# SyncE's transfers in the written order through the attention stage of a hybrid encoder block

## The chip, the cores and the metric

The kernel runs on one core of a Trainium2 chip. The metric is the device time of one execution in microseconds (us). A core has five engines with queues of their own: TensorE (PE; its weight loads are shown apart as PEld), VectorE (DVE), ScalarE (ACT), GpSimd (POOL) and SyncE (SP), which computes nothing and here issues nearly all DMA transfers. Each engine runs its instructions in the order of its queue: where one waits for a semaphore, what stands behind it waits too.

## What is computed

One layer on x of 2048 tokens by 1024, cut to its core:

```python
h = rmsnorm(x, norm_mix_g)
proj = h @ w_in                              # u_ssm 512 | q 512 | k 512 | v 512
y_ssm = s5_mixer(u_ssm, ...)                 # diagonal complex state space, GELU, GLU
y_att = chunked_attention(q, k, v, rel_bias) # 8 heads of 64; a chunk of 64 tokens sees
                                             # itself and the 8 chunks before it
x = x + concat(rmsnorm(y_ssm), rmsnorm(y_att)) @ w_out
x = x + (silu(h2 @ w_gate) * (h2 @ w_up)) @ w_down     # h2 = rmsnorm(x), 2816 wide
return rmsnorm(x, norm_final_g)
```

Products that need float32 accuracy are made of three: each operand is kept as a rounded part and a remainder (hi, lo), and hi*hi, hi*lo and lo*hi are added (`mm3`).

## The kernel before

The program is written for a framework that takes the instructions in the order in which Python emits them, and then schedules each engine's queue with a timing model: an instruction that is ready earlier by the model may be put ahead of its written place. Buffers are named pools with a number of slots; a tile that needs a slot waits for the last use of the tile that had it. `keep_in_program_order` pins an instruction behind the one that was emitted before it on its engine. `Ordered` (line 68) does so for all matmuls, so PE runs in written order. `Pinned` (81) wraps another engine in the same way: `k.V`, `k.A`, `k.Q` are the pinned DVE, ACT and SP; `nc.vector`, `nc.scalar`, `nc.sync` are the free ones.

The stages: projection of u (`u_phase`, with `ssm_prologue` beside it), attention with the state-space units beside it (`att_phase`, the one that changes), the mix and output projection (`mix_phase`), and the feed-forward part (`gate_up_phase`, `down_phase`).

`att_phase` works on 4 blocks of 512 tokens (sb 0 to 3). Its loop (line 956) runs 128 steps and a few more; step s = 32 sb + 8 pr + 4 hh + qp handles head 2 pr + hh and the tile qp of 128 queries. In a step are emitted, in this order: the scores of step s (two or four matmuls, tile `sc`), the transposes of step s-2, at the end of a head its product with v, and then the next pieces of the *units*, which prepare what later steps need. A unit is a Python generator, advanced so that its pieces spread evenly over a given range of steps; it is started two to four steps earlier, so that its first loads are asked for. For block sb, counted from step 32 sb:

- `hT_unit`: loads 8 input tiles (`xt`, 256 KB each, 2 buffers, line 722), normalises them on DVE (736), and makes hi on ACT (737) and lo on DVE (728). Tiles 0 to 2 start at -14, tiles 3 to 7 at -10, with their first two loads; from -8 on they take the buffers of the block before, which PE reads until about step -9.
- `qk_unit` (q and k of a pair of heads; from steps -8, 2, 7 and 19) and `v_unit` (v of four heads; from -2 and 13). Each uses two weights `w` of 1 MB, in 3 buffers. In block 0 they are loaded raw, split (ACT, DVE) and stored to `wss`; later blocks load them from there (705). They are asked for at -11, 32 sb + 0, 5 and 17 for `qk_unit` and at -4 and 11 for `v_unit`.
- q of a pair goes from PSUM to `q2h` and `q2l` (777, 778; 3 buffers, one for each head), and a copy by DMA fills their other half (779, 780). k goes to `k2`, is stored (`ks`, 785) for the next block, and the part of `k2` with the block before's keys, the *kept keys*, is loaded (755).
- A bias tile `nb` (320 KB) is loaded for the next head in each step with qp = 2 (825). The result of a pair of heads is stored as `ya_s` (907) at steps 3, 11, 19, 27.
- Eight `ssm_unit`s, every 14 steps, load `U`, `Bst`, `Tm`, `Vm` in many small transfers (568), scan on POOL, and store `y` (660).

At step 119 (`OPEN`, line 957) buffers are released and the first part of `mix_phase` joins as one more unit. In `weight_steps` (line 1277), far behind, four DRAM-to-DRAM copies of 512 KB of w_down into `wt` go through `k.Q`.

Of SP's instructions in `att_phase` before the change, those of state-space unit 0, of `hT_unit` for block 0 and of weights 0 and 4 are pinned; the rest are free.

Of the kernel before, what the change touches and what calls it, by code (L numbers as in the profile page):

```python
# [16 lines left out]
P = 128  # L17
# [3 lines left out]
NG, CH, NS = 32, 16, 64  # L21
# [58 lines left out]

class Pinned:


    def __init__(self, tc, eng):
        self.tc, self.eng = tc, eng

    def __getattr__(self, name):
        f = getattr(self.eng, name)
        return lambda *a, **b: self.tc.keep_in_program_order(f(*a, **b))  # L89


class K:
    def __init__(self, tc, io):
        self.tc, self.nc, self.io = tc, tc.nc, io
        self.n = 0
        self.te = Ordered(tc)
        self.ta = self.te if PINA else tc.nc.tensor
        self.V, self.A, self.Q = (Pinned(tc, e) for e in (tc.nc.vector, tc.nc.scalar, tc.nc.sync))
# [9 lines left out]
def f32(ap):  # L108
    return ap.bitcast(F32)
# [451 lines left out]
def ssm_unit(k, p, psum, S, b, eng):  # L561
# [3 lines left out]
    U = k.t(p, "U", [P, GB, NC], bufs=2)  # L565

    def load(out, in_):
        ins = nc.sync.dma_start(out, in_)
        if b == 0:
            k.tc.keep_in_program_order(ins)  # L570

    for j in range(L):
        load(U[j * CH : (j + 1) * CH], S["u"][b * F : (b + 1) * F, j, :].rearrange("(g c) t -> c g t", c=CH))
# [77 lines left out]
    for q in range(GP):  # L651
        ps = k.t(psum, "pj", [P, 2, NC], bufs=2)
        for g2 in range(2):
            g = 2 * q + g2
            k.ta.matmul(ps[:, g2, :], tm[:, g, :], U[:, g, :], start=True, stop=False)
            k.ta.matmul(ps[:, g2, :], vm[:, g, :], XG[:, g, :], start=False, stop=True)
        nc.scalar.copy(Y[:, 2 * q : 2 * q + 2, :], ps[:])
        if q == GP - 1:
            for j in range(L):
                nc.sync.dma_start(S["y"][b * F : (b + 1) * F, j, :].rearrange("(g c) t -> c g t", c=CH), Y[j * CH : (j + 1) * CH])  # L660
        yield


# [25 lines left out]
def att_phase(k, ident, S):  # L689
    tc, nc, io = k.tc, k.nc, k.io  # L690
    with ExitStack() as cx:
# [3 lines left out]
        def load_w(sb, n):  # L695

            w = k.t(aw, "w", [P, 2, 1024], F32R, bufs=WB)
            if sb == 0:
                raw = k.t(aw, "raw", [P, 1024], bufs=2)
                pin = n in (0, 4)  # L700
                (k.Q if pin else nc.sync).dma_start(raw[:], io["w_qk"][n] if n < 8 else io["w_v"][n - 8])
                split(k, w[:, 0], w[:, 1], raw[:], k.V if pin else k.wlo_eng, k.A if pin else None)
                keep[n] = w
            else:
                nc.sync.dma_start(f32(w[:]), S["ws"][n])
            return w[:, 0], w[:, 1]

        def keep_w(n):
            if n in keep:
                (k.Q if n in (0, 4) else nc.sync).dma_start(S["ws"][n], f32(keep.pop(n)[:]))  # L710

        def hT_unit(sb, q0=0, q1=KT):
            hi, lo = hT.setdefault(sb, ([], []))
            ts = slice(sb * SB, (sb + 1) * SB)
            xts = {}
            V, A, Q = (k.V, k.A, k.Q) if sb == 0 else (nc.vector, nc.scalar, nc.sync)

            def load(q):
                if q < q1:
                    x = RING[q] if sb == 0 and q < 2 * DB else None  # L720
                    xts[q] = k.t(aw, x, [P, SB]) if x else k.t(aw, "xt", [P, SB], bufs=XB)
                    Q.dma_start(xts[q][:], io["xt"][q * P : (q + 1) * P, ts])

            ahead = 2 if sb else KT
            for q in range(q0, q0 + ahead):
                load(q)
            def low(q):
                V.tensor_tensor(lo[q][:], xts[q][:], f32(hi[q][:]), op=ALU.subtract)

            for q in range(q0, q1):  # L730
                yield
                load(q + ahead)
                xt = xts[q]
                for v, n in zip(hT[sb], ("hi", "lo")):
                    v.append(k.t(aw, f"{n}{q}x" if q < DB and sb % 2 else f"{n}{q}", [P, SB], F32R))
                V.scalar_tensor_tensor(xt[:], xt[:], k.gm[:, q : q + 1], S["rsn"][:, ts], op0=ALU.mult, op1=ALU.mult)
                A.copy(hi[q][:], xt[:])  # L737
                if sb == 0 and q:
                    low(q - 1)
                if sb or q == KT - 1:  # L740
                    low(q)
            yield

        def qk_unit(sb, pr):
# [5 lines left out]
            else:  # L750
                ts = [(k.t(aa, "q2h", [P, SB], F32R, bufs=3), k.t(aa, "q2l", [P, SB], F32R, bufs=3), k.t(aa, "k2", [P, 2 * SB], F32R, bufs=3)) for _ in range(2)]
            qk[sb, pr] = ts
            if sb > 0:
                for hh in range(2):
                    nc.sync.dma_start(f32(ts[hh][2][:, :SB]), S["k"][(sb - 1) % 2, 2 * pr + hh])
            both = (sb, pr) == (0, 0)
            pss = []
            for c in range(2):
                if c == 0 or not both:
                    cc = range(2) if both else (c,)  # L760
                    pss += [k.t(pfs, "pf", [P, 512]) for _ in cc]
                    for q in range(KT):
                        cs = slice(q * P, (q + 1) * P)
                        for m in cc:
                            wh, wl = ws[m]
                            mm3(k.ta, pss[m][:], wh[:, cs], wl[:, cs], hi[q][:], lo[q][:], q == 0, q == KT - 1)
                            if q == 2:
                                keep_w(4 * m + pr)
                        if q < KT - 1:
                            yield  # L770
                ps = pss[c]
                for hh in range(2):
                    q2h, q2l, k2 = ts[hh]
                    a = slice(hh * 64, hh * 64 + 64)
                    o = slice(64 - hh * 64, 128 - hh * 64)
                    if c == 0:
                        nc.scalar.activation(q2h[a, :], ps[a, :], AF.Copy, scale=-0.125)
                        nc.vector.scalar_tensor_tensor(q2l[a, :], ps[a, :], -0.125, f32(q2h[a, :]), op0=ALU.mult, op1=ALU.subtract)
                        nc.sync.dma_start(f32(q2h[o, :]), f32(q2h[a, :]))
                        nc.sync.dma_start(f32(q2l[o, :]), f32(q2l[a, :]))  # L780
                    else:
                        nc.scalar.copy(k2[a, -SB:], ps[a, :])
                        nc.vector.tensor_tensor(k2[o, -SB:], ps[a, :], f32(k2[a, -SB:]), op=ALU.subtract)
                        if sb < NSB - 1:
                            nc.sync.dma_start(S["k"][sb % 2, 2 * pr + hh], f32(k2[:, -SB:]))
                yield

        QK_N = 1 + 2 * KT
# [110 lines left out]
        def pv_scale(st):  # L899
# [7 lines left out]
            nc.sync.dma_start(S["ya"][sb, pr * P : (pr + 1) * P, :], ya[:])  # L907
# [798 lines left out]
```

## Time and profile before

| | |
|---|---|
| median of the three runs shown | 2344.45 us |
| the three runs | 2341.79, 2353.02, 2344.45 us |
| the profiled execution, its own time | 2347.47 us |
| its span, first to last instruction | 2345.7 us |
| mean granted PE clock | 0.969 |
| attention steps 0 to 127, first score matmuls | 142.5 to 770.8 us |

The profile is of one execution. A row of the timeline reads: start in us from the span's start, length in us, engine (SPq is SP's queue), source line, operation, output tile <- input tiles, shape, count of merged instructions, and in brackets the idle time of the engine before it and what ended it. Line 75 is the helper `Ordered.matmul`, so all of PE's matmuls bear it, and line 89 that of `Pinned`. The chain of work that ended last is followed back from the end; its rows give start, length and what ran, a transfer from its issue to its landing. A row of the waits reads: who waited, for whom, us in total, number of times, longest. SP's own waits are counted from the end of its instruction before.

### The profile page before, as it was taken

Reading aid. Unit: us, or ns where it says so; the run is one execution under the profiler, and the core shown is the slowest. Engines: PE = TensorE matmul, PEld = TensorE weight load, DVE = VectorE, ACT = ScalarE, POOL = GpSimd, SP = SyncE. Lnnn points to the kernel's source line nnn. Section 1 sums busy time; section 2 is a strip of 40 time slices with the busy share of each in tenths; the row PEclk is TensorE's granted clock in tenths of the full one; section 3 lists DMA queues with packets and bytes.
Section 4 is the critical chain, followed back from the end, with each engine's and each line's share of the span. In section 5 each row is a group of like instructions: output and inputs, shape, how many; then the busy total and the mean of one; then the engine's idle time right before and its main releaser. Section 6 shows DMA issues by size and latency. Waiting matters only on the chain.

```text
span 2345.7 us, 30460 instructions
## 1 busy us (share of the span) xinstructions
PE 2198.3 (94%) x10568; PEld 1843.6 (79%) x10568; DVE 1511.7 (64%) x2332; ACT 996.8 (42%) x1696; POOL 1023.7 (44%) x1225
## 2 busy tenths in 40 slices
PE   8978689898997799989999999999999999999997
PEld 6676578788886688778888888788888878888886
DVE  7944545555556876765776578766645376579676
ACT  5345445555455643153333335433333343345322
POOL 3406655354550022145555555455555415345442
PEclk9988799999998999999999999999999999999998
DMA  8786666666655324663554646654433197565551
GB/s 297 257 283 201 196 206 200 179 196 200 201 160 160 130 90 157 216 222 97 188 172 163 224 164 227 244 191 164 162 108 106 57 332 264 182 208 189 193 193 73
DMA packets 216371, 437.01 MB, mean 186 GB/s; under 512 B 27352, under 2 KB 58120, under 8 KB 209112
## 3 DMA queue, kind: packets, MB, share of 16 engines
q1 hardware_dynamic: 211352, 420.89, 53.7%
q0 software_dynamic: 4864, 14.17, 1.9%
q8 instruction: 83, 1.36, 0.2%
q14 instruction: 72, 0.59, 0.1%
HBM read 294.98 MB, written 132.15 MB: 182 GB/s over the span
## 4 chain that ended last, share of the span: by engine, by line
PE 73%; DVE 9%; issue 6%; DMA 6%; POOL 3%; ACT 3%; SPq 1%; DVEq 0%; POOLq 0%; ACTq 0%
PE X L75 19%; PE ps L75 18%; PE Y L75 9%; PE pf L75 7%; PE big L75 7%; PE W L75 5%; PE pj L75 4%; PE sc L75 2%; PE pt L78 2%; DMA xt<-in_xt 2%; DMA w<-wss 1%; DVE lo L167 1%; DVE acc L1576 1%; ACT X L597 0%; DVE cm L89 0%
## 5 line engine op out<-in xcount | busy, mean ns | idle before, releaser
L75 PE MATMUL X<-hi,c 128*128 128x512 f32 x1408 | 451.8, 392 | 6.8 <-DMA hq<-g 3.4
L75 PE MATMUL ps<-hd,hd 128*128 128x512 f32 (+1 forms) x1968 | 431.8, 381 | 3.8 <-DVE hd L167 3.7
L75 PEld LDWEIGHTS ps<-hd,hd 128*128 128x128 f32 x1968 | 358.8, 190 | 75.4 <-DVE hd L167 5.3
L167 POOL TENSOR_TENSOR c<-S,c 128x512 fp32r<-128x512 f32 x176 | 254.2, 1446 | 259.8 <-ACT c L166 256.0
L75 PEld LDWEIGHTS X<-hi,c 128*128 128x128 f32 x1408 | 265.9, 189 | 64.3 <-ACT u L1392 4.9
L75 PE MATMUL X<-lo,c 128*128 128x512 f32 x704 | 275.1, 391 | 0.0
L167 POOL TENSOR_TENSOR hd<-hd 128x1536 fp32r<-128x1536 f32 (+1 forms) x46 | 161.6, 3517 | 229.3 <-ACT hd L166 220.8
L167 POOL TENSOR_TENSOR c<-raw,c 128x512 fp32r<-128x512 f32 x132 | 189.1, 1432 | 137.7 <-ACT c L166 106.4
L166 ACT CAST hd<-hd 128x1536 fp32r<-128x1536 f32 (+1 forms) x106 | 147.4, 1393 | 219.2 <-DMA hd<-hq 152.0
L75 PE MATMUL Y<-hi,c 128*128 128x512 f32 x704 | 226.1, 392 | 5.2 <-DVE u L1396 5.2
L1522 DVE TENSOR_TENSOR acc<-acc,ps 128x512 f32<-128x512 f32 x196 | 129.2, 682 | 77.9 <-PE ps L75 77.6
L75 PE MATMUL pf<-hi,w 128*128 128x512 f32 x416 | 154.7, 424 | 16.9 <-ACT hi L737 10.2
L75 PE MATMUL big<-m,woh 128*128 128x512 f32 x512 | 163.2, 401 | 0.0
L75 PEld LDWEIGHTS Y<-hi,c 128*128 128x128 f32 x704 | 133.0, 189 | 34.5 <-DVE u L1396 6.8
L854 DVE CUSTOM_DVE_ANT_0 s<-sc,nb 128x640 f32<-128x640 f32 (+4 forms) x128 | 94.5, 739 | 100.5 <-PE sc L75 95.2
L166 ACT CAST c<-S 128x512 fp32r<-128x512 f32 x176 | 109.3, 621 | 117.5 <-PE Y L75 58.5
L75 PEld LDWEIGHTS X<-lo,c 128*128 128x128 f32 x704 | 132.8, 189 | 27.4
L1392 ACT COPY u<-X 128x512 f32<-128x512 f32 x132 | 77.0, 584 | 175.2 <-PE X L75 175.2
L611 POOL TENSOR_TENSOR st<-X,a 128x128 f32<-128x128 f32 (+2 forms) x136 | 47.9, 352 | 234.3 <-ACT X L597 224.3
L166 ACT CAST c<-raw 128x512 fp32r<-128x512 f32 x132 | 82.1, 622 | 146.4 <-PE Y L75 80.3
L167 DVE TENSOR_TENSOR hd<-hd 128x1536 fp32r<-128x1536 f32 (+1 forms) x60 | 119.6, 1995 | 32.6 <-ACT hd L166 32.0
L75 PE MATMUL Y<-lo,c 128*128 128x512 f32 x352 | 137.7, 391 | 0.0
(456 smaller groups left out, 4648.3 us busy)
## 6 DMA issues: line engine op xcount, KB each, us to landing
w<-wss SPq DMA_DIRECT2D x36, 1024.0 KB, 6.4
hq<-g SPq DMA_DIRECT2D x140, 256.0 KB, 2.1
hd<-hq SPq DMA_DIRECT2D x42, 768.0 KB, 4.5
hd<-wc SPq DMA_DIRECT2D x42, 768.0 KB, 6.1
raw<-in_w_gate SPq DMA_DIRECT2D x44, 512.0 KB, 3.6
raw<-in_w_up SPq DMA_DIRECT2D x44, 512.0 KB, 4.0
wc<-px SPq DMA_DIRECT2D x66, 256.0 KB, 3.2
wss<-w SPq DMA_DIRECT2D x12, 1024.0 KB, 6.7
```

Source lines behind the costliest of these rows:

```text
L75: return self.tc.keep_in_program_order(self.tc.nc.tensor.matmul(*a, **b))
L78: return self.tc.keep_in_program_order(self.tc.nc.tensor.transpose(*a, **b))
L166: (hi_eng or nc.scalar).copy(hi, raw)
L167: (lo_eng or nc.gpsimd).tensor_tensor(lo, raw, f32(hi), op=ALU.subtract)
L611: eng.tensor_tensor(t[:, :, :, :n], src, ar, op=ALU.mult)
L854: nc.vector.tensor_tensor_reduce(s[:, :nk].rearrange("p (a b) -> p a b", a=nch), ps[:, :nch, :half], hd.nb[:, nk - 1 :: -1].rearrange("p ( ...
L1392: nc.scalar.copy(u[:], ps[:])
L1522: V.tensor_tensor(a, a, ps[:], op=ALU.add)
L1576: nc.vector.scalar_tensor_tensor(v, v, k.go[:, i : i + 1], self.rs[:, : self.n], op0=ALU.mult, op1=ALU.mult)
```

## The change

All of SP's transfers that are emitted in `att_phase` up to step 119 go through the pinned `k.Q`, so that SP runs them in the order in which they are written. At step 119 `Pinned.free` is set, and from there `k.V`, `k.A` and `k.Q` pin nothing. In `hT_unit`, for blocks 1 to 3, the load of tile q + 2 is emitted behind the work on tile q, which has the buffer that it takes; before, it was emitted ahead of it. In `qk_unit` the load of each head's kept keys is emitted behind the two copies of that head's q, instead of at the unit's start.

```diff
 class Pinned:
+    free = False
...
     def __getattr__(self, name):
         f = getattr(self.eng, name)
-        return lambda *a, **b: self.tc.keep_in_program_order(f(*a, **b))
+        return f if self.free else lambda *a, **b: self.tc.keep_in_program_order(f(*a, **b))
...
 # ssm_unit
     def load(out, in_):
-        ins = nc.sync.dma_start(out, in_)
-        if b == 0:
-            k.tc.keep_in_program_order(ins)
+        k.Q.dma_start(out, in_)
...
-                nc.sync.dma_start(S["y"][b * F : (b + 1) * F, j, :]...
+                k.Q.dma_start(S["y"][b * F : (b + 1) * F, j, :]...
...
 # load_w, keep_w
-                (k.Q if pin else nc.sync).dma_start(raw[:], io["w_qk"][n] if n < 8 else io["w_v"][n - 8])
+                k.Q.dma_start(raw[:], io["w_qk"][n] if n < 8 else io["w_v"][n - 8])
-                nc.sync.dma_start(f32(w[:]), S["ws"][n])
+                k.Q.dma_start(f32(w[:]), S["ws"][n])
-                (k.Q if n in (0, 4) else nc.sync).dma_start(S["ws"][n], f32(keep.pop(n)[:]))
+                k.Q.dma_start(S["ws"][n], f32(keep.pop(n)[:]))
...
 # hT_unit
-            V, A, Q = (k.V, k.A, k.Q) if sb == 0 else (nc.vector, nc.scalar, nc.sync)
+            V, A, Q = (k.V, k.A, k.Q) if sb == 0 else (nc.vector, nc.scalar, k.Q)
...
                 yield
-                load(q + ahead)
+                if sb == 0:
+                    load(q + ahead)
                 xt = xts[q]
...
                     low(q)
+                if sb:
+                    load(q + ahead)
...
 # qk_unit
-            if sb > 0:
-                for hh in range(2):
-                    nc.sync.dma_start(f32(ts[hh][2][:, :SB]), S["k"][(sb - 1) % 2, 2 * pr + hh])
...
-                        nc.sync.dma_start(f32(q2h[o, :]), f32(q2h[a, :]))
-                        nc.sync.dma_start(f32(q2l[o, :]), f32(q2l[a, :]))
+                        k.Q.dma_start(f32(q2h[o, :]), f32(q2h[a, :]))
+                        k.Q.dma_start(f32(q2l[o, :]), f32(q2l[a, :]))
+                        if sb > 0:
+                            k.Q.dma_start(f32(k2[:, :SB]), S["k"][(sb - 1) % 2, 2 * pr + hh])
...
-                            nc.sync.dma_start(S["k"][sb % 2, 2 * pr + hh], f32(k2[:, -SB:]))
+                            k.Q.dma_start(S["k"][sb % 2, 2 * pr + hh], f32(k2[:, -SB:]))
...
 # load_nb, pv_scale
-            nc.sync.dma_start(nb[:], S["nbm"][h])
+            k.Q.dma_start(nb[:], S["nbm"][h])
-            nc.sync.dma_start(S["ya"][sb, pr * P : (pr + 1) * P, :], ya[:])
+            k.Q.dma_start(S["ya"][sb, pr * P : (pr + 1) * P, :], ya[:])
...
 # the loop
             if s == OPEN:
+                Pinned.free = True
                 aw.release()
```

More of the change, by code (lines that the diff above doesn't have):

```diff
@@ L95, in __init__ @@
         self.n = 0
+        Pinned.free = False
         self.te = Ordered(tc)
@@ L659, in ssm_unit @@
             for j in range(L):
-                nc.sync.dma_start(S["y"][b * F : (b + 1) * F, j, :].rearrange("(g c) t -> c g t", c=CH), Y[j * CH : (j + 1) * CH])
+                k.Q.dma_start(S["y"][b * F : (b + 1) * F, j, :].rearrange("(g c) t -> c g t", c=CH), Y[j * CH : (j + 1) * CH])
         yield
```

## Prediction

> **What bounds the kernel now.** I read the page first, for the engine that carries the span. The rows give busy time and share of the span by engine, then the share of the chain that ended last.
>
> ```profile
> PE 2198.3 (94%) x10568; PEld 1843.6 (79%) x10568; DVE 1511.7 (64%) x2332; ACT 996.8 (42%) x1696; POOL 1023.7 (44%) x1225
> ...
> PE 73%; DVE 9%; issue 6%; DMA 6%; POOL 3%; ACT 3%; SPq 1%; DVEq 0%; POOLq 0%; ACTq 0%
> ```
>
> TensorE (PE) is the bound: busy in 94% of the span, and 73% of the chain are its instructions. Only what makes PE wait, or lets it wait less, moves the time. The change touches the stage in which the 128 attention steps run. So the next view was busy time by stretch: three stretches in which one block of 512 tokens gives way to the next, and a quiet one (columns: PE, weight loads, DVE, ACT and POOL busy, PE's granted clock, DMA share, GB/s).
>
> ```profile
> 252.60:316.40 63.80, 44.11 (x211) 35.23 (x210) 30.72 (x64) 25.61 (x65) 21.61 (x54) 0.84 0.67 212
> 409.80:470.80 61.00, 50.77 (x282) 44.18 (x281) 36.61 (x61) 31.40 (x62) 22.61 (x50) 0.92 0.64 179
> 568.60:624.00 55.40, 49.41 (x282) 43.73 (x280) 33.78 (x56) 30.05 (x60) 37.87 (x88) 0.94 0.71 204
> 624.00:685.80 61.80, 60.00 (x370) 54.10 (x369) 33.13 (x59) 33.72 (x67) 29.52 (x82) 1.00 0.57 177
> ```
>
> In the quiet stretch PE lacks 1.8 us of 61.8. In the three changes of block it lacks 19.7, 10.2 and 6.0 us, together 35.9, and the granted clock falls to 0.84, 0.92 and 0.94. These three are where the order of SP's transfers can be felt. The view of the waits, for PE alone over the whole stage, says what ended them (total, times, longest):
>
> ```profile
> PE sc L75 <- DVE k L783: 11.8, 3, 7.3
> ...
> PE pf L75 <- DMA w<-wss: 10.5, 5, 3.5
> PE pf L75 <- ACT hi L737: 10.2, 5, 3.8
> ...
> PE pf L75 <- DVE lo L728: 5.6, 5, 2.1
> ...
> PE pj L75 <- DMA XG<-X: 3.7, 1, 3.7
> ```
>
> Weights that have not landed (10.5 us), input blocks not yet normalised and split (ACT hi and DVE lo, 15.8 us), keys that DVE has not written (11.8 us). All three hang on when a transfer was asked for. SP's own waits show the candidate for the gain: the loads of kept keys.
>
> ```profile
> SPq L755 <- PE sc L75: 67.1, 13, 11.3
> ```
>
> SP stood 67.1 us, in 13 places, in front of a load of kept keys (line 755) whose buffer was still read by scores; everything behind it in the queue stood too. That is what the move of this load takes away. The question is whether PE ever waited for what stood behind it, and what the written order does to the other loads.
>
> **The change part by part.** Step numbers are those of the loop (front section); I set them beside the trace by counting the 448 score matmuls.
>
> *Kept keys.* Their load now stands behind the four copies of q in the same unit. The second head's q buffer comes free with the same scores as its key buffer, so its copies wait where the load waited: in the written order SP still stands at that place, only for line 779 in place of 755. No instruction is added or dropped. Value taken: 0 by itself.
>
> *Input tiles.* Within a unit no other SP instruction lies between the old place of the load and the new one; the load waits for the same release of its buffer. Value taken: 0.
>
> *The written order.* This is the part with a price. Before, the scheduler could put a load ahead of its place when its buffer was free. The first change of block already runs in nearly the written order, so its rows show what that costs (SP's issues, then a piece of the chain):
>
> ```profile
> 254.97 1.23 SPq L705 DMA_DIRECT2D w<-wss  x2
> ...
> 257.30 1.34 SPq L722 DMA_DIRECT2D xt<-in_xt  x2
> ...
> 257.30 11.36 DMA xt<-in_xt
> ```
>
> Two weights of 1 MB, a bias tile and a 1 MB store go ahead of the two input tiles, which land 13.7 us after the first weight was asked for. It is the change with the most PE idle, 19.7 us. The written order makes the other two more like it. Term by term:
>
> 1. First block, value unit of the upper heads. Its two raw weights were asked for ahead of the second head's q copies; written, they stand behind the store of step 11:
>
> ```profile
> 188.44 0.98 SPq L701 DMA_DIRECT2D raw<-in_w_v  x1
> ...
> 197.47 0.58 SPq L701 DMA_DIRECT2D raw<-in_w_v  x1
> ...
> 203.38 0.33 SPq L907 DMA_DIRECT2D ya_s<-ya  x1
> ...
> 208.99 0.48 PE L75 MATMUL pf<-w,hi 128*128 128x256 f32 x2
> ```
>
> From 203.8 on, two transfers of 0.5 MB and two splits reach PE's need at 208.99 about 2 to 5 us late. PE's next wait, 3.7 us for XG (quoted above), depends on POOL and not on PE, and takes up most of it. Taken: +0.5 (0 to +2).
>
> 2. Second block, first value unit. Six of the eight U loads were issued in gaps before its weights; written, all eight and Bst stand between the q copies and the weights:
>
> ```profile
> 274.90 0.91 SPq L568 DMA_DIRECT2D U<-u  x2
> ...
> 280.75 2.89 SPq L568 DMA_DIRECT2D U<-u  x4
> ...
> 295.13 0.98 SPq L705 DMA_DIRECT2D w<-wss  x2
> ...
> 295.61 10.37 DMA w<-wss
> ...
> 302.14 0.50 PE L75 MATMUL pf<-w,hi0x 128*128 128x256 f32 x2 [2.73 <-DMA w<-wss]
> ...
> 306.02 0.51 PE L75 MATMUL pf<-w,hi 128*128 128x256 f32 x2 [2.19 <-DMA w<-wss]
> ```
>
> PE already waits 2.73 + 2.19 us here. Six issues of 0.46 us (0.91 for two) are 2.8, and a second kept-key load 0.35: taken +3.2 (0 to +4).
>
> 3. Third block, input tiles. The two weights were asked for at 403 and 408 (5.69 us for both), ahead of the q copies; written they follow the copy at 413.90:
>
> ```profile
> 403.24 5.69 SPq L705 DMA_DIRECT2D w<-wss  x2
> ...
> 413.90 0.46 SPq L780 DMA_DIRECT2D q2l<-q2l  x1
> ...
> 415.11 1.05 SPq L722 DMA_DIRECT2D xt<-in_xt  x2
> ...
> 424.51 1.42 DVE L736 SCALAR_TENSOR_TENSOR xt<-xt,g_mix,rsn 128x512 f32<-128x512 f32 x2 [5.70 <-DMA xt<-in_xt]
> 425.96 0.68 DVE L783 TENSOR_TENSOR k<-pf,k 64x512 fp32r<-64x512 f32 x1
> ```
>
> By the first change, less the 1 MB store's share of its 3.8 MB (3.6 of 13.7 us), the tiles land 10.1 us after 414.4, so at 424.5, as now; the two kept-key loads (0.5 MB) ahead add up to 1.8. Against it stands that DVE ran the two input products before the key (424.51, then 425.96) and stood 5.70 us for them; that is the longest of the key waits (7.3). With later tiles the scheduler, whose DVE order stays free, may put the key first; PE then loses part of it at the tiles instead. Taken: +1 for the tiles here, +1 in the fourth block, -2 for the keys (-7.3 to +8 in all).
>
> 4. Third block, first value unit: the first of its weights was asked for at 432.25, the second as soon as a buffer came free. Written, both stand behind the store at 456.31:
>
> ```profile
> 432.25 0.38 SPq L705 DMA_DIRECT2D w<-wss  x1
> ...
> 456.31 0.37 SPq L907 DMA_DIRECT2D ya_s<-ya  x1
> ...
> 463.80 0.48 PE L75 MATMUL pf<-w,hi 128*128 128x256 f32 x2
> ```
>
> Issued at about 457, the first lands near 464, level with 463.80, by the 7.18 us of term 5's last row; the second, at 10.4 us as in the pair of term 2, lands at 467.6, and PE wants it 12 matmuls (some 1.5 us) after 463.80. Taken: +2.3 (0 to +4). In the fourth block PE comes later against the same place: 0.
>
> 5. Third and fourth block, second value unit. The first weight was asked for early, the second behind the same step's store, and PE waited for the second:
>
> ```profile
> 508.22 0.42 SPq L705 DMA_DIRECT2D w<-wss  x1
> ...
> 671.40 0.45 SPq L705 DMA_DIRECT2D w<-wss  x1
> ...
> 527.77 7.63 DMA w<-wss
> ...
> 677.80 7.18 DMA w<-wss
> ```
>
> Written, both are asked for there together. The second of a pair took 10.4 us, against 7.63 and 7.18 for these alone; with its issue half a microsecond later that is +3.3 and +3.7, taken 3.5 each (0 to +5 each).
>
> Sum: 0.5 + 3.2 + 1 + 1 - 2 + 2.3 + 3.5 + 3.5 = **+13.0 us**. The cover is none: PE is the bound and has no other work in program order. What goes away early does not come back later, since after the stage the chain is again PE.
>
> *The switch to free order at step 119.* Behind it SP's few bias loads and stores are unpinned as before. But the four copies of w_down into wt were pinned too, and are not any more:
>
> ```profile
> L89 SPq DMA_DIRECT2D wt<-in_w_down x4: 581/588/590, 1304.6 to 1306.5; - x4
> ...
> DMA to landing us min/median/max: 4.3/8.0/10.6
> ```
>
> They wait for no buffer and no result, so they may float to wherever SP first finds nothing else ready. From their own landing, in the worst case they push 8 us of other transfers; where those have slack, nothing. Taken 0 (0 to +8).
>
> The profiled execution took 2347.47 us, its span 2345.7 with 1.8 outside it; the median of the three runs shown is 2344.45, 3.0 less. I add the sum to the median: 2344.45 + 13 = 2357.
>
> **The clock, weighed.** The first change of block has a granted clock of 0.84, the quiet stretch 1.00. [...]
>
> **The rivals.**
>
> *Hidden anyway.* SP has waited for the same q copies all along, and the weights that lose their lead had slack. For it: term 4 lands its first weight in time, and stretches between the changes lack under 2 us. Against: PE waits on weights now, in five places. The time would be 2344 to 2350.
>
> *Faster: the keys first.* With SP in written order DVE's order follows, and the key writes no longer stand behind input products. The price is in the waits: 11.8 us for keys, and some of the 15.8 for input blocks. It decides if DVE runs both keys of a block's last unit before the next input tile lands, and the weights of terms 4 and 5 still land in time: 2344 - 12 = 2332. Against it: the first change of block has this order already, and lacks most.
>
> *Not quite what it says: the four copies.* If they float into the start or into a change of block, +8 on top: 2365.
>
> *Deeper clock dips.* If the longer idles cost as the first change does, where 63.8 us at 0.84 is 10 us of clock beside 19.7 us of idle, it is a half more on the sum: 2344 + 19 = 2363. [...]
>
> **How the numbers follow.** Forecast (slower, 2350 to 2368) 0.46; hidden 0.26; faster 0.14; four copies 0.09; clock 0.05. About 0.5% (12 us) is what a measurement of this kernel can tell from no change. Two thirds of the forecast's share lie over 2356, with the last two rivals 0.46 slower; the rest of it and nearly all of the second rival 0.40 same; 0.14 faster. The range takes in the floor of the keys' term with all others at 0 (-7.3) and reaches up to the upper ends of most terms with the four copies: 2336 to 2380.
>
> **What would show it.** Right: PE's wait for w<-wss grows from 10.5 to 20 or more; both weights of each second value unit issued within 1 us of each other; line 755 hardly waits and line 779 waits instead; the stretches of the three changes longer by 3 to 6 us. Wrong: the key waits vanish and the tiles do not wait in their place, or the weight loads still land before PE asks, or wt's copies appear elsewhere with PE waiting beside them.

## The result and the profile after

The changed kernel took 2373.78 us (median of 6 runs, 2370.14 to 2390.99) and the kernel before 2345.61 us beside it (6 runs, 2339.6 to 2353.02): a ratio of 1.0129, with a 95% interval of 1.0094 to 1.0165 (over all runs; the two medians alone give 1.0120). By the medians that is 28 us slower, where the prediction had +13.

The page of the changed kernel, busy time by engine and the shares of the chain:

```profile
PE 2209.8 (93%) x10568; PEld 1848.1 (78%) x10568; DVE 1508.4 (64%) x2332; ACT 999.5 (42%) x1696; POOL 1021.8 (43%) x1225
...
PE 73%; DMA 8%; DVE 8%; issue 4%; ACT 3%; SPq 2%; POOL 1%; DVEq 0%; POOLq 0%; ACTq 0%
```

PE is still the bound, with the same 10568 matmuls in the same order, but DMA has gone from 6% to 8% of the chain, and PE is busy for 11.5 us more. Because PE's order is the same, its stretches can be matched matmul by matmul. Busy time by stretch, for the kernel before: the stage from the first score matmul of step 0 to that of step 127, what follows it, and two stretches between changes of block (columns: PE, weight loads, DVE, ACT, POOL busy, PE's granted clock, DMA share, GB/s):

```profile
142.48:771.37 628.89, 552.72 (x3216) 488.70 (x3216) 339.86 (x651) 321.93 (x680) 292.80 (x708) 0.93 0.62 189
771.37:996.58 225.21, 208.78 (x944) 171.22 (x943) 166.65 (x328) 90.39 (x141) 39.82 (x28) 0.96 0.46 154
316.52:409.82 93.30, 89.88 (x575) 81.59 (x573) 53.11 (x99) 51.08 (x105) 63.86 (x167) 1.00 0.62 194
470.91:568.72 97.81, 92.54 (x587) 84.73 (x585) 50.45 (x92) 49.69 (x101) 52.92 (x135) 0.98 0.65 203
```

The same for the changed kernel, with the three changes of block and the quiet stretch of the prediction among them, in order of time:

```profile
143.94:790.96 647.02, 560.35 (x3215) 490.49 (x3216) 341.99 (x651) 324.13 (x680) 293.93 (x708) 0.92 0.59 185
790.96:1021.80 230.84, 211.38 (x944) 173.18 (x943) 165.75 (x328) 90.40 (x141) 41.51 (x28) 0.94 0.45 149
250.40:314.69 64.29, 45.77 (x210) 36.34 (x210) 29.94 (x63) 25.50 (x65) 23.13 (x60) 0.81 0.65 189
314.69:410.98 96.29, 91.44 (x574) 82.73 (x572) 52.45 (x98) 50.22 (x102) 63.84 (x167) 0.98 0.58 183
410.98:475.04 64.06, 51.03 (x281) 42.62 (x282) 35.28 (x59) 31.91 (x62) 26.14 (x67) 0.95 0.66 201
475.04:580.88 105.84, 96.42 (x587) 87.72 (x585) 52.33 (x96) 51.06 (x101) 49.41 (x118) 0.94 0.56 172
580.88:638.60 57.72, 50.72 (x283) 43.77 (x281) 34.69 (x57) 30.41 (x59) 38.38 (x88) 0.91 0.65 209
638.60:705.11 66.51, 62.37 (x369) 55.66 (x368) 32.93 (x59) 34.19 (x67) 33.31 (x86) 0.96 0.58 179
```

Three things are to be seen. **First**, the stage is 18.1 us longer. Of that, 10.5 us are idle time of PE (647.02 - 560.35 = 86.7, against 628.89 - 552.72 = 76.2), and 7.6 us are PE itself, which needs 560.35 us for the matmuls that took 552.72: the same work at a lower granted clock, 0.92 against 0.93 over the stage. **Second**, most of the time is not where I looked. Beside the stretches of before, the three changes of block are longer by 0.5, 3.1 and 2.3 us; the stretches between them by 3.0, 8.0 and, the one called quiet, 4.7 us. The first stretch, from step 0 to the first change of block, is shorter by 3.7 us (106.46 against 110.12). **Third**, 5.6 us arose behind the stage, where the change does nothing. All of this compares two single profiles; a second profile of the kernel before, below, moves some of these figures.

PE's waits in the stage, of the changed kernel:

```profile
PE pf L75 <- DMA w<-wss: 17.5, 7, 6.9
PE sc L75 <- DVE mn L856: 14.4, 10, 3.7
PE pf L75 <- ACT hi L738: 13.3, 7, 3.6
PE pf L75 <- ACT w L168: 11.3, 3, 5.3
PE pt L78 <- DVE ptl L875: 9.6, 10, 2.9
...
PE sc L75 <- DVE k L785: 5.4, 3, 2.3
```

Weights: 17.5 us against 10.5. The key waits are halved, 11.8 to 5.4, though most of that fall is no effect of the change (second profile, below). The other rows have grown: input blocks (hi) from 10.2 to 13.3, the splits of raw weights (w L168) from 6.0 to 11.3, scores waiting for the work on earlier scores (mn) from 10.9 to 14.4, and probabilities (ptl) from 7.1 to 9.6. The prediction had named the first two of these.

### The profile page after: what moved, and what is told of

The parts are those of the page before. It is cut to its first block, busy times and chain, and to the rows that moved or that the text cites. A ratio compares the mean times of both kernels' runs of the same rounds, so it can differ in the third digit from the quotient of the medians.

```text
span 2373.2 us, 30455 instructions
## 1 busy us (share of the span) xinstructions
PE 2209.8 (93%) x10568; PEld 1848.1 (78%) x10568; DVE 1508.4 (64%) x2332; ACT 999.5 (42%) x1696; POOL 1021.8 (43%) x1225
## 4 chain that ended last, share of the span: by engine, by line
PE 73%; DMA 8%; DVE 8%; issue 4%; ACT 3%; SPq 2%; POOL 1%; DVEq 0%; POOLq 0%; ACTq 0%
PE X L75 19%; PE ps L75 18%; PE Y L75 9%; PE pf L75 8%; PE big L75 7%; PE W L75 5%; PE pj L75 4%; PE sc L75 2%; DMA w<-wss 2%; PE pt L78 2%; DMA xt<-in_xt 2%; SPq L90 1%; DVE lo L169 1%; DVE s L856 1%; DVE acc L1579 1%
## 5 line engine op out<-in xcount | busy, mean ns | idle before, releaser
L168 ACT CAST hd<-hd 128x1536 fp32r<-128x1536 f32 (+1 forms) x106 | 147.4, 1393 | 221.3 <-DMA hd<-hq 169.2
L75 PE MATMUL pf<-hi,w 128*128 128x512 f32 x416 | 154.5, 423 | 23.1 <-ACT hi L738 13.3
L168 ACT CAST c<-S 128x512 fp32r<-128x512 f32 x176 | 109.5, 622 | 118.7 <-PE Y L75 56.6
L75 PEld LDWEIGHTS X<-lo,c 128*128 128x128 f32 x704 | 133.0, 189 | 27.5
L875 DVE TENSOR_TENSOR ptl<-pt,pth 128x640 fp32r<-128x640 f32 (+3 forms) x152 | 98.4, 648 | 73.5 <-ACT pth L874 71.9
L168 ACT CAST c<-raw 128x512 fp32r<-128x512 f32 x132 | 82.1, 622 | 143.0 <-PE Y L75 80.9
L859 ACT ACTIVATE s<-s,mn 128x640 f32<-128x640 f32 (+4 forms) x128 | 97.9, 765 | 96.0 <-DVE mn L856 95.1
```

The lines of the kernel that those rows point to most:

```text
L75: return self.tc.keep_in_program_order(self.tc.nc.tensor.matmul(*a, **b))
L168: (hi_eng or nc.scalar).copy(hi, raw)
L859: nc.scalar.activation(s[:, :nk], s[:, :nk], AF.Exp, bias=mn[:], scale=-1.0, accum_out=sums[sb, pr][:, hh, qp : qp + 1])
L875: nc.vector.tensor_tensor(ptl[:, a:b, qp, :], pt[:, a:b, :], f32(pth[:, a:b, qp, :]), op=ALU.subtract)
```

## The experiments

Four theories were tested. **A**: the loss is made of single transfers that stand in SP's written order behind waits that are not theirs. **B**: the moves, or DVE's order, which the scheduler makes anew each time, are the cause. **C**: any written order loses this much, because SP stands in front of the first wait. **U**, formed later: the written order holds back two kinds of loads with opposite effects, U (a gain) and weights with bias tiles (a loss). Each ratio is against the kernel before on the same chip in the same job. The expectations are quoted as they were written, and their letters shift: in the first two, B is that the moves carry the price; C is the loss through the four copies of w_down in the first and in the one on these copies, and any written order in the one on U; D and R are rivals named on the spot.

| kernel | median us | ratio to before | 95% interval |
|---|---|---|---|
| changed kernel | 2373.78 | 1.0129 | 1.0094 to 1.0165 |
| moves only, order free | 2345.65 | 0.9992 | 0.9965 to 1.0018 |
| order only, no moves | 2393.49 | 1.0183 | 1.0133 to 1.0234 |
| changed, weights free | 2358.10 | 1.0055 | 1.0030 to 1.0079 |
| changed, wt copies pinned | 2373.71 | 1.0105 | 1.0050 to 1.0160 |
| changed, weights and bias tiles free | 2333.02 | 0.9948 | 0.9930 to 0.9967 |
| changed, bias tiles free | 2364.35 | 1.0077 | 1.0056 to 1.0098 |
| changed, U asked for earlier | 2357.19 | 1.0049 | 1.0031 to 1.0067 |
| before, once more | 2346.72 | 1.0007 | 0.9986 to 1.0028 |
| changed, weights, bias tiles and U free | 2349.08 | 1.0013 | 0.9996 to 1.0030 |
| before, moves, U pinned | 2326.97 | 0.9930 | 0.9908 to 0.9952 |
| weights and bias tiles free, U earlier | 2349.50 | 1.0025 | 1.0010 to 1.0039 |
| before, U pinned | 2331.70 | 0.9943 | 0.9924 to 0.9962 |

### The two moves, and the order without them

The first kernel is the one before with the two moves and its free order (the new line is `nc.sync.dma_start` there):

```diff
             for q in range(q0, q1):
                 yield
-                load(q + ahead)
+                if sb == 0:
+                    load(q + ahead)
...
+                if sb:
+                    load(q + ahead)
...
-            if sb > 0:
-                for hh in range(2):
-                    nc.sync.dma_start(f32(ts[hh][2][:, :SB]), S["k"][(sb - 1) % 2, 2 * pr + hh])
...
+                        if sb > 0:
+                            nc.sync.dma_start(f32(k2[:, :SB]), S["k"][(sb - 1) % 2, 2 * pr + hh])
```

> The kernel before with the two moves alone: input tiles and kept keys asked for behind the last use of their buffers, SP's order left to the scheduler. Theory A (the price of the change is the written order): 0 us, within 5, against the kernel before. Rival B (the moves carry the price, since the kept keys come behind the copies of q): +10 us or more. Rival C (the price is in the lost pin of the four copies of w_down and the free order behind step 119): 0 as well, since neither is in this kernel.

The second is the changed kernel with both moves undone and everything pinned.

> The changed kernel with the two moves undone: all of SP's transfers of the stage in written order, kept keys asked for at the unit's start, input tiles ahead of the work on the tile before. Theory A: as slow as the changed kernel (+28) or slower, up to +45, as SP then stands at the kept keys from the unit's start, two to three steps earlier than at the copies of q. Rival B: faster than the changed kernel by 10 us or more.

The moves alone measure as nothing (0.9992, interval on both sides of 1). The order alone gives 1.0183 against 1.0129 for the whole change (four runs only; by its median it is 46 us slower than before, 1 us past the expected +45); the intervals overlap a little, the medians lie 20 us apart. So the loss comes from the pinning, and the moves, if anything, soften it. SP's waits in that kernel say how: its largest row is SP in front of kept keys again, as before the change (67.1 us then), but now everything stands behind it.

```profile
SPq L90 <- PE sc L75: 83.3, 11, 16.2
```

### Weights free, bias tiles free, both free

```diff
 # load_w, first and third kernel
-                k.Q.dma_start(raw[:], io["w_qk"][n] if n < 8 else io["w_v"][n - 8])
+                (k.Q if pin else nc.sync).dma_start(raw[:], io["w_qk"][n] if n < 8 else io["w_v"][n - 8])
...
-                k.Q.dma_start(f32(w[:]), S["ws"][n])
+                nc.sync.dma_start(f32(w[:]), S["ws"][n])
...
 # load_nb, second and third kernel
-            k.Q.dma_start(nb[:], S["nbm"][h])
+            nc.sync.dma_start(nb[:], S["nbm"][h])
```

> The changed kernel with the loads of the attention weights (raw and kept, lines 701 and 705) free again, all else in written order. Theory A: PE's wait for w<-wss falls from 17.5 us to under 8, the raw weights' stall of 5.3 + 1.0 us goes, the steps' end comes 10 to 16 us earlier, and the time is +10 to +18 us against the kernel before. Rival D (the bias tiles and input tiles behind SP's waits carry it): +23 or more, with PE waiting elsewhere.

> The change, but with the bias tile loads alone in free order. Theory A: the waits of scores for mn (14.4 us in all in the changed kernel, 3.9 us at the upper heads' value unit of the third block) shrink to about the 10.9 us of before, the weight waits of 17.5 us stay: 3 to 7 us less than the changed kernel, 2367 to 2371. Theory B: no change beyond 3 us, 2371 to 2377, since PE meets the weights a little later at the same places.

> The change, but with the weight loads (lines 701, 705) and the bias tile loads (line 826) in free order; U, the input tiles, the q copies, the kept keys and the stores stay in the written order. Theory A (the loss is made of single transfers that wait in SP's written order behind waits that are not theirs, and each PE stall has its own such transfer): the waits of scores for DVE's mn of 1.5, 3.9 and 2.5 us that the run with free weights kept all follow from a bias tile asked for late, so they go; about 6 to 9 us less than with free weights alone (2358), 2347 to 2352. Theory B (what is left is not the bias tiles, but DVE's own order, which the scheduler makes anew with each change): the mn waits move to another place, and the time stays within 4 us of 2358.

By the ratios, freeing the weights takes back 0.0074 of the 0.0129 (17 us), freeing the bias tiles 0.0052 (12 us), and freeing both 0.0181 (42 us), more than the two together; that kernel is faster than the kernel before, with all other transfers still in the written order. The first came out as expected (2358.10, +11 us by the medians of its job, with the end of the steps 12.8 us earlier). The second was better than the expected 2367 to 2371, and not as described: PE's mn waits fell to 6.4 us, below the 10.9 of before, while its waits for weights rose to 24.1 us.

For both together theory A had the direction and far too small a size, and one of its reasons was wrong. I had blamed three waits for mn on late bias tiles. With both free, the longest of them (3.7 us) is still there, and mn waits add up to 15.1 us, against 20.1 with the weights alone free. A free load can be left where it was: in that kernel SP still issues this bias tile (509.96) right behind the same kept keys (509.33). PE's waits, of the kernel with weights alone free and then of the one with both:

```profile
PE sc L75 <- DVE mn L856: 20.1, 10, 3.7
```

```profile
PE sc L75 <- DVE mn L856: 15.1, 7, 3.7
...
PE pf L75 <- DMA w<-wss: 0.2, 1, 0.2
```

The wait for weights is 0.2 us in both, so it does not explain the 25 us between these two. Between them PE's idle time in the stage falls from 78.5 to 61.2 us and the time of its matmuls from 557.2 to 546.0, with a little less in many rows: mn, input blocks (hi 14.0 to 11.0), keys (10.2 to 8.0), XG (3.8 to 0.5). Why freeing the bias tiles brings so much more beside free weights is not shown. What both show is that PE waits 0.2 us for weights where the kernel before had 10.5 with its weights as free as here. That was the lead to theory U.

### The wt copies

```diff
-        k.Q.dma_start(S["wt"][m], k.io["w_down"][f * P : (f + 1) * P, :])
+        k.tc.keep_in_program_order(nc.sync.dma_start(S["wt"][m], k.io["w_down"][f * P : (f + 1) * P, :]))
```

> The changed kernel with the four copies of w_down pinned again, where the kernel before had them; PE, DVE, ACT and POOL run in the same order as in the changed kernel. Theory A: the first matmul of step 0 comes 1.4 us earlier, at 142.5, and the time falls by 1 to 3 us: +25 to +27 against the kernel before. Rival C: the 7 us that the changed kernel loses behind the attention steps go as well: +19 or less.

They did float: the tile's row in the changed kernel has them near the start, 1250 us earlier than before.

```profile
L1280 SPq DMA_DIRECT2D wt<-in_w_down x4: 501/564/632, 49.8 to 70.4; - x4
```

Pinned again, the kernel takes 2373.71 us: the copies cost nothing that can be measured, with four runs and an interval of 1.0050 to 1.0160. The expected earlier start did not come either: the first matmul of step 0 stands at 144.5 us, against 143.9 in the changed kernel and 142.5 expected.

### U asked for earlier in the written order

```diff
-            units.append(Unit(ssm_unit(...), SSM_N if b else SSM_N + YL - 1, s0, s0 + SPAN, 4 if b else 0, light=SL))
+            units.append(Unit(ssm_unit(...), SSM_N if b else SSM_N + YL - 1, s0, s0 + SPAN, 8 if b else 0, light=SL))
```

> The change, everything in the written order as it is, but the U loads (and Bst) of the blocks after the first stand four steps earlier in it: 8 steps ahead of their unit in place of 4, so that they are asked for ahead of the q copies. Theory A (the place in the queue makes the loss, not that the order is kept): the wait of 6.95 us for the first value unit's weights of the second block falls back to 2 to 4 us, and the new wait of 2.8 us in the third block's qk unit of the second pair goes; with the clock 5 to 10 us less than the changed kernel, 2364 to 2369. Against it the U loads now stand ahead of the input tiles of the first change of block, 0.5 MB or about 2 us there. Theory C (any written order loses the same, since the loss comes from SP standing in front of the first wait): within 3 us of 2374.

One number of the code is changed, all else is pinned as in the change, and the ratio goes from 1.0129 to 1.0049. In the second block the weights no longer stand behind U, and PE, which had waited 6.95 us there, waits 0.63 (SP's issues, then PE's matmuls; the profiled execution took 2348.1 us, the fastest of the 12 runs, so its rows show the place and not the size):

```profile
288.98 0.95 SPq L90 DMA_DIRECT2D w<-wss  x2
```

```profile
294.62 0.51 PE L75 MATMUL pf<-w,hi0x 128*128 128x256 f32 x2 [0.63 <-DMA w<-wss]
```

Theory C falls: a written order with another place for one kind of load loses a good half less. Its gain, 17 us by medians, is above the expected 5 to 10. (With this edit the scheduler also put 31 of DVE's some 650 instructions in the stage in another order; what that brought is not separated.)

### The kernel before, once more

> The kernel before once more, without an edit, for its profile. The stretch behind the attention stage took 225 us up to PE's next wait in the profiled execution before and 229 to 231 in all others, the one with nothing changed on average too. If that is how two executions of one program differ, this profile shows 228 to 231 there, and a stage of 626 to 632 us. If it is caused by the changes, 224 to 226.

```profile
142.75:762.93 620.18, 551.09 (x3215) 487.27 (x3216) 337.96 (x651) 322.00 (x680) 293.53 (x708) 0.93 0.62 192
762.93:993.08 230.15, 212.40 (x944) 174.32 (x943) 166.44 (x328) 90.39 (x141) 41.56 (x28) 0.93 0.45 150
```

The stretch behind the stage took 230.2 us here and 225.2 in the first profile of the same program; the changed kernel's 230.8 is close to the one here. The 5.6 us behind the stage are therefore no effect that these profiles can give to the change. The stage itself, where 626 to 632 us had been expected, differs by 8.7 us between the two executions, so differences of single profiles of this size prove nothing, and the verdicts above rest on the ratios.

Some readings of the first profile change with this one. PE's waits for keys:

```profile
PE sc L75 <- DVE k L783: 7.7, 3, 3.3
```

The wait of 7.3 us, the longest in the first profile, is 3.3 here, and with the moves alone the key waits are 6.8 us. So of the fall from 11.8 to 5.4 us in the changed kernel only the part from about 7 can be the change's. Set against this profile, the changed kernel's stage is 26.8 us longer, of which 17.6 are idle time of PE and 9.3 its matmuls; the three changes of block are longer by 1.1, 7.8 and 2.5 us, and the stretches between them by 3.6, 8.2 and 5.3. That the greater part lies between the changes of block holds against both profiles.

### U held back, weights free

With weights and bias tiles free, U was now freed as well (`nc.sync` for blocks after the first in `ssm_unit`'s `load`):

> Free weight loads and bias tiles as in the run that came out at 2333, and the U loads and Bst of the blocks after the first free as well; input tiles, q copies, kept keys and stores stay in the written order. Theory U (the gain over the kernel before comes from holding the U loads back: there they slip in ahead of weights that PE needs sooner, and with U in the written order they cannot): with U free the first value unit of the second block waits for w again, 2 to 5 us, and the time goes back most of the way, 2340 to 2347. Theory R (the gain comes from the written order of the rest: input tiles and q copies ahead of everything else): 2331 to 2336.

And to the kernel before with the moves, only this was added, then to the kernel before itself:

```diff
     def load(out, in_):
-        ins = nc.sync.dma_start(out, in_)
-        if b == 0:
-            k.tc.keep_in_program_order(ins)
+        k.Q.dma_start(out, in_)
```

> The kernel before with the two moves (which alone came out at a ratio of 0.999), and of all transfers in the attention stage that were free, only the U loads and Bst in the written order. Theory U: this alone brings the gain, 2332 to 2339, with the waits of the second block's first value unit for w gone (4.9 us before). Theory R: 2342 to 2350, as with the moves alone.

> The kernel before, where it is written, with one thing changed: the U loads and Bst of the blocks after the first keep the written order, as those of the first block do already. Input tiles and kept-key loads stand where they stood before. Theory U with the moves worth nothing (as alone, ratio 0.999): 2322 to 2333, as with the moves and U pinned (2327). Rival: with U held in place, SP's waits in front of the kept keys (67 us before) are what U and all behind it stand behind, so the moves matter here: 2336 to 2348.

And the earlier place for U was tried on the version with weights and bias tiles free:

> The version at 2333 (weights and bias tiles free, the rest written), with the U loads and Bst standing four steps earlier in the written order. Theory U: they stand ahead of the first change of block's input tiles again and no weight gains, so no gain here although the same edit took 16 us from the full written order: 2332 to 2342. If the two edits add up: about 2320.

The three that free or pin U came out as theory U had it, two of them past the end of its range (2349.08 where 2340 to 2347 was expected, 2326.97 below its 2332); with U free PE waits 2.6 and 0.6 us for the second block's weights again. The fourth was expected to bring no gain, and it lost: the earlier place, which took 17 us from the full written order, added 16 here (2349.5, expected at most 2342), so the two edits don't add up. PE's waits there have 7.3 us for weights, against 0.2 without the edit, and 20.4 for mn, against 15.1.

Freeing U turns 0.9948 into 1.0013; pinning U alone, in the kernel before, gives 0.9943, and with the moves 0.9930. Matched matmul by matmul, the gain with weights and bias tiles free arises in two places, both early. From step 0 to the first change of block, with U free and then with U pinned:

```profile
145.43:253.59 108.16, 92.29 (x485) 79.28 (x486) 49.27 (x117) 51.71 (x133) 57.95 (x126) 0.87 0.64 216
```

```profile
143.89:244.11 100.22, 89.52 (x486) 76.76 (x487) 47.09 (x116) 51.70 (x133) 53.91 (x113) 0.90 0.70 228
```

That is 7.9 us less; the first change of block with the value unit at its end takes 59.1 us in place of 63.6, and the rest of the stage taken together about the same. In the first of the two places PE's wait for XG goes, with U free and then pinned:

```profile
PE pj L75 <- DMA XG<-X: 3.3, 1, 3.3
```

```profile
PE pj L75 <- DMA XG<-X: 0.5, 1, 0.5
```

In the two profiles of the kernel before this wait is 3.7 and 4.1 us, and with U alone pinned it has no row. In these kernels with U free, SP issues the stores of two weights of 1 MB behind U, at 214 to 217 us, while XG's transfers are under way; in those with U pinned they go out ahead of U, at 203 to 210 us. XG's transfers take up to 7.1 us to land in the first profile of before, and up to 3.4 with the moves and U pinned. The kernel with weights alone free fits: U is pinned there, yet the stores stand behind it at 214.6 us, and PE waits 3.8 us for XG. That XG is late because of these stores is read from the rows and not tested.

In the second place, before the second block's first value unit, U stands ahead of weights. With U free, its loads are dotted over the gaps, and the two weights are asked for together at the end:

```profile
280.51 1.83 SPq L570 DMA_DIRECT2D U<-u  x4
...
293.56 0.97 SPq L705 DMA_DIRECT2D w<-wss  x2
```

With U pinned (weights and bias tiles free in both), the gaps fall to the weights, and U goes behind the q copies:

```profile
260.99 0.32 SPq L705 DMA_DIRECT2D w<-wss  x1
...
279.47 0.33 SPq L705 DMA_DIRECT2D w<-wss  x1
...
284.26 5.83 SPq L90 DMA_DIRECT2D U<-u  x8
```

The fastest version, the kernel before with the moves and U pinned, has the shortest stage, and PE waits for weights once there, 3.1 us:

```profile
143.19:749.36 606.17, 545.64 (x3216) 482.25 (x3217) 337.52 (x651) 321.88 (x680) 292.04 (x708) 0.95 0.64 197
```

So the change is two opposite things in one. The rest of the pinning (input tiles, q copies, kept keys, stores), with the moves and the free order behind step 119, costs nothing that can be measured (1.0013, with U, weights and bias tiles free). Holding U back then gains about 0.65%, and holding weights and bias tiles back behind it loses about 1.8%. These shares hold for this order of taking the kinds apart: weights and bias tiles freed one by one gave 17 and 12 us, together 42.

## Why the prediction was right in its sign and short in its size

*Kept keys and input tiles, 0 each.* Right: 0.9992 for the moves alone.

*Term 1, raw weights of block 0, +0.5 behind the cover of XG.* The stall is where it was forecast, and longer. PE now waits

```profile
208.63 0.58 PE L75 MATMUL pf<-w,hi 128*128 128x256 f32 x1 [5.29 <-ACT w L168]
```

and 1.04 us more at the next one, 6.3 us, and the cover, 3.7 us of waiting for XG, was used up: its row is gone from the waits. But this is not what the term cost. PE was ready for these weights at 203.3, 59.4 us behind step 0, where it wanted them 66.5 us behind step 0 before: earlier waits had shrunk, among them one for mn from 3.8 to 1.2 us, and one for ptl of 1.8 us had gone. The stall ate this lead. The stretch from step 0 to the first change of block takes 106.5 us, against 110.1 and 108.4 in the two profiles of before, and 105.7 with the weights free, where this stall is gone. By that last pair, two single profiles, holding the raw weights back cost about 0.8 us in this stretch, close to the 0.5 taken, but by a stall of 6.3 us and a lead that was not foreseen.

*Term 2, second block's first value unit, +3.2.* Right to a few tenths. SP's issues and PE's waits:

```profile
287.92 3.79 SPq L90 DMA_DIRECT2D U<-u  x8
...
292.88 0.96 SPq L90 DMA_DIRECT2D w<-wss  x2
```

```profile
300.35 0.80 PE L75 MATMUL pf<-w,hi0x 128*128 128x256 f32 x2 [6.95 <-DMA w<-wss]
...
304.20 0.51 PE L75 MATMUL pf<-w,hi 128*128 128x256 f32 x2 [0.92 <-DMA w<-wss]
...
465.60 0.51 PE L75 MATMUL pf<-w,hi 128*128 128x256 f32 x2 [1.42 <-DMA w<-wss]
...
469.35 0.51 PE L75 MATMUL pf<-w,hi 128*128 128x256 f32 x2 [2.05 <-DMA w<-wss]
...
509.29 0.79 PE L75 MATMUL pf<-hi,w 128*128 128x512 f32 x1 [2.81 <-DMA w<-wss]
...
541.13 0.60 PE L75 MATMUL sc<-k,q2h 128*128 128x320 f32 x1 [3.68 <-DVE mn L856]
```

6.95 + 0.92 against 2.73 + 2.19 before is +2.95 (+3.7 against the second profile, where the two waits are 2.73 and 1.43).

*Term 3, tiles and keys, 0 in all.* Key waits fell from 11.8 to 5.4 us and the waits for hi rose from 10.2 to 13.3, about half of it given back. But the -2 was read off a wait of 7.3 us that the second profile of the same program has at 3.3, so most of the fall would be there without any change, and the rows do not show that the rival "keys first" happened.

*Term 4, third block's first value unit, +2.3.* 1.42 + 2.05 = 3.5, the two rows at 465.60 and 469.35: above the 2.3, inside its 0 to +4.

*Term 5, second value units, +3.5 each.* Both weights were issued together, as predicted:

```profile
535.57 0.96 SPq L90 DMA_DIRECT2D w<-wss  x2
```

(in the fourth block at 694.42, 0.95 us for both). But in the third block PE came late itself, by a wait of 3.68 us for mn (the row at 541.13), and no longer waited for the weight, so that one wait took the place of another as long (3.5 us before). In the fourth block the wait for weights did not grow, 1.64 us against 1.80 before. PE's lag behind the kernel before grows by 2.3 us across the unit's matmuls there, in place of 3.5, because they start at a granted clock of 0.50 (701.10 to 706.60 us), where it was 1.00 before.

*Missed.* The term 2 pattern a second time: U, Bst, then two weights for the third block's second pair. This is the wait of 2.81 us at 509.29, in a stretch where I expected nothing; the same edit of U's place took both away. I had counted the value units and left the qk units out.

```profile
500.06 3.77 SPq L90 DMA_DIRECT2D U<-u  x8
...
504.33 0.91 SPq L90 DMA_DIRECT2D w<-wss  x2
```

*The sum.* My 13 us were idle time of PE. In the stage it grew by 10.5 us against the first profile of the kernel before and by 17.6 against the second. That 13 lies between is partly luck: term 5 gave about 2 of its 7 us, and waits that no term had, such as the one at 509.29, made up for it. The step that failed is the one on the clock: rival "deeper clock dips" stood at 0.05 and the forecast itself took nothing for it. The stage's matmuls took 7.6 us more at the lower clock (9.3 against the second profile), 0.7 us for each us of idle, or 0.5 by the second profile; the rival had said half. Against the second profile, idle time and clock together are 26.8 of the 29.4 us by which the spans differ. Against the first they are 18.1 of 27.5, and the rest, 5.6 behind the stage and some 4 around it, is of the size by which the two profiles of the kernel before differ.

The signs that I had named were right for the weights of the second value units and for kept keys: SP's waits of the changed kernel have only 0.9 us left for scores, in place of 67.1 before, but a larger row for q in front of its copies (40.3 us before).

```profile
SPq L90 <- ACT q2h L777: 79.6, 19, 8.7
```

They were wrong for the waits on w (17.5, not 20), and for the three changes of block (longer by 0.5 to 3.1 us against the first profile and by 1.1 to 7.8 against the second, not 3 to 6 each).

Not tried: DVE's and ACT's order held still while only SP's changes. The traces show how far that order moved within the stage. Of some 650 instructions of DVE, 51 stand in another order in the changed kernel than before, and 23 to 54 between the two kernels of each experiment that frees, pins or shifts a kind of load (ACT's order moves by much the same). It moved little where only the moves or the copies of w_down differ: 5 for the moves alone, none for the copies, and 6 between the changed kernel and the order without moves. These two lie 20 us apart, so a difference of that size needs no new order on DVE. How much of the mn, hi and ptl waits is made by the scheduler's new order on DVE, and how much by late transfers, these runs don't separate.

## What to carry to other kernels

A queue order isn't good or bad as a whole: ask, for each kind of transfer, what it would be put in front of and what it would be put behind. Here one kind that needed no lead (U) had been taking the gaps in which more urgent transfers (weights) could be asked for; to pin that one kind was worth 0.6 to 0.7%, to pin all cost 1.3%. When a bound engine is predicted to wait longer, count the slower clock behind the wait as a term of its own (here 0.5 to 0.7 us for each us of idle), and go through every unit that loads the delayed tile, not only those that wait already. Price no single wait from one profile: take a second profile of the same program first. And ask of a longer wait whether the engine only came to it earlier.

## What the hardware showed that I had not expected

A wait of 2.81 us was followed by half the clock, and for longer than the wait. Busy time by stretch of the changed kernel, ahead of the wait at 509.29 and behind it:

```profile
500.00:505.76 5.76, 5.76 (x37) 5.26 (x36) 2.34 (x4) 2.58 (x5) 0.00 (x0) 1.00 0.67 200
509.29:512.00 2.71, 2.71 (x6) 2.14 (x7) 0.00 (x0) 0.59 (x1) 0.00 (x0) 0.50 0.99 304
512.00:514.50 2.50, 2.50 (x9) 2.15 (x8) 0.00 (x0) 0.00 (x0) 0.00 (x0) 0.50 0.82 310
514.50:517.00 2.50, 2.50 (x13) 2.25 (x12) 1.46 (x3) 1.35 (x3) 0.00 (x0) 0.81 0.01 2
```

The clock is 1.00 up to the stretch that holds the wait, 0.50 for at least the 5.2 us behind it, and then comes back: some 2.6 us lost in these 5.2 us, behind 2.81 us of waiting. The length of the wait alone doesn't decide it. In the same kernel a wait of 2.93 us left the clock at 1.00:

```profile
574.80 0.77 PE L78 MATMUL pt<-ident,s 128*128 128x128 f32 x5 [2.93 <-DVE ptl L875]
```

```profile
574.80:578.80 4.00, 4.00 (x24) 3.59 (x25) 3.13 (x6) 1.62 (x3) 0.00 (x0) 1.00 0.60 193
```

and behind one of 2.32 us, which ended at 597.72, it was 0.50 for the next 3 us. Behind the 6.95 us of term 2 it was 0.50 for the next 2.1 us and 1.00 again from 304.20. What decides it, these runs don't show. Over nine profiles of the stage PE's idle time and the time of its matmuls go together: from the fastest version to the order without moves,

```profile
142.50:809.73 667.23, 568.13 (x3216) 497.28 (x3216) 342.76 (x651) 323.84 (x680) 291.68 (x708) 0.91 0.58 180
```

PE's idle time grows by 38.6 us (60.5 to 99.1) and the time of the same matmuls by 22.5 (545.64 to 568.13), 0.6 us for each us of idle.
